# A transformer layer's feed-forward start: one token tile handled in two halves, transposes and operand splits moved in a written-out order

## The chip, the cores and the metric

One core of a Trainium2 chip runs the whole layer in one launch. The metric is the device time of one execution in microseconds (us), the median over several runs. The core's engines are TensorE (PE, with its weight loads PEld), VectorE (DVE), ScalarE (ACT), GpSimd (POOL) and SyncE (SP, which issues nearly all DMAs here).

## The reference

One layer of a backbone with 640 tokens (512 latent tokens in four tiles of 128, and one tile of 128 context tokens), width 1024, feed-forward width 2816. Two attention-like branches (a bidirectional recurrence and a neighbourhood attention) are merged; what matters here is what follows them:

```python
x = x + g1 * (merged @ p["w_out"])
h2 = _rmsnorm(x, p["norm2_g"]) * (1.0 + sc2) + sh2
x = x + g2 * ((jax.nn.silu(h2 @ p["ffn_w1"]) * (h2 @ p["ffn_w3"])) @ p["ffn_w2"])
```

`g1`, `sc2`, `sh2`, `g2` come from the conditioning vector, one set for the latent tokens and one for the context tokens.

## The kernel before

**Numbers.** Every large matrix product is made of three TensorE passes: an operand is split into a rounded high part, which ACT casts, and a low part, the difference, which DVE (or POOL) subtracts; the passes are high x high, high x low and low x high. `split` (L203 to L205) does this for activations, `wcast` (L185, L188) and `w_hl` (L1851, L1854) for weights. So each operand costs one ACT instruction, then one DVE instruction that waits for it.

**The stage.** The last part of the `w_out` product runs token tile by token tile (`acc`, L303), first tiles 0, 1, 2 together (72 matmuls), then tiles 3 and 4 (48). As a tile's product ends, `n_add` adds it to `x2`, `n_square`, `n_rstd` and `n_scale` normalise the tile, `n_out` transposes it on TensorE (L1739; four 128x128 blocks for each half `q` of the width, into a PSUM tile `xt` of a ring of three) and ACT (L1745) and DVE (L1747) scale and shift it out of PSUM into `hq[q, n]`, two blocks each; `n_split` splits that into `B2[q, n]`, high and low. `n` is the half of the tokens: 0 for tokens 0 to 319, 1 for 320 to 639. Token tile 2 lies across the border, so `cuts(2)` gives two pieces of 64 tokens.

**The first two hidden tiles** (`ft` 0 and 1) use `B2` directly: `conv_gen(ft, n)` makes two products, with `w1` and `w3`, of 24 matmuls each, in the order (0, 0), (1, 0), (0, 1), (1, 1). Their weights are `ffw[0]` to `ffw[3]`. `conv_out` applies silu (L1833, on ACT), multiplies (L1834, DVE) and splits the result into `u`. The tiles after them go through `pair`: seven products stand for eight, over sums and differences of weights (`w_sum`, L1865: `s1` to `s4`) and differences of the token halves. `t_sum` (L1769) makes these four differences in place in `hq`, `t_split` splits them into `BT[1]` to `BT[4]`. The weight operands of a pair are called a, b, c, d; `ha`, `la` are the high and low part of a, and so on.

**A detail of `pair`.** Its products run in the order a, b, a, b, c, b, c (the fourth b-type one uses weight d). The first a product ends in PSUM tile `A_`; ACT copies it out (`p1`, L1891), and the third product then adds on into the same `A_`. So the third product may start only when the copy `p1` has been made. In the table `wt`, `hc` (an ACT cast) stands ahead of `p` on ACT.

**The order.** TensorE, DVE, ACT and POOL run in the order in which the code emits. `beside` counts the matmuls of this stage and calls, at the numbers of the table `n2`, the steps that stand there, each a letter and an index:

| letter | step |
|---|---|
| A, S, R, X | `n_add`, `n_square`, `n_rstd`, `n_scale` of a token tile |
| T, U | `n_out` of a tile, width half 0 and 1 |
| H, J | `n_split` of a tile, width half 0 and 1 |
| W | load and split one of the weights `ffw` |
| D, E | `t_sum`, `t_split` |
| Y | `conv_out` (index 2 ft + n) |
| K | K0 issues the DMAs of the first pair's weights, K1 to K8 take the entries of `w0` in turn |

Matmuls 1 to 72 are tiles 0 to 2 of `w_out`, 73 to 120 tiles 3 and 4, 121 to 168 `conv_gen(0, 0)`, 169 to 216 `conv_gen(1, 0)`, 217 to 264 and 265 to 312 the two with n = 1. The four `hq` tiles and the two parts of `B2[0, 1]` lie in a ring "q" of six buffers, whose buffers the `u` tiles take over later in the order in which they were handed out.

Of the kernel before, what the change touches and what calls it, by code (L numbers as in the profile page):

```python
# [7 lines left out]
F32 = mybir.dt.float32  # L8
# [6 lines left out]
P = 128  # L15
NT = 640
NS = 512
H2 = 320
# [36 lines left out]
        "2 0 6 6 6 4 4 5 2 0 5 1 1 0 0"),  # L55
    qp=((0, 0, 7, 6, 7), (2, 5, 4, 4, 3, 2, 5, 3, 1)), ada=2, pa=1, pd=0,
    lw=(0, 0, 0, 0, 0, 2, 2, 2, 2, 2, 2, 2, 2, 2, 2, 2),
    n2=("48:A0S0 60:A1S1R0X0 72:A2S2R1X1 74:R2T0 76:U0X2H0J0 86:T1U1H1J1 89:W1 92:W0 100:T2U2H2J2 108:A3S3 "
     "120:A4S4R3X3R4X4W2W3 160:T3U3H3J3 180:T4U4H4J4 200:D1D3D2D4 210:E2E3E1 218:K0E4 "
     "230:Y0Y2K1K2K3K4K5K6K7K8 266:Y1"),  # L60
    te="dddddddd", pf=2, se="pddd", oe="d", w0="s3 s1 s2 s4 ha la hb lb",
    wt=(
        "<x -hc <h p -hd -lc <m",
        "u -ld <i <o",
# [43 lines left out]
def body(ctx: ExitStack, tc: tile.TileContext, xs, xp, cols, consts, w_ada, b_row, w_rw, w_qkv,  # L108
# [69 lines left out]
    def wcast(w, eng=None):  # L178
        st, n, pl, nhl = w
        hi = pl.tile([P, 1024], F32R, tag="whi", bufs=nhl, name=nm("whi"))  # L180
        lo = pl.tile([P, 1024], F32R, tag="wlo", bufs=nhl, name=nm("wlo"))
        if eng is pool:
            act.activation(lo[:, :n], st[:, :n], AF.Copy, scale=-1.0)
            pool.dma_start(lo[:, :n].bitcast(F32), st[:, :n], accum_op=ALU.add)
        act.copy(hi[:, :n], st[:, :n])  # L185
        if eng is not pool:
            def low(a, b):
                dve.tensor_tensor(out=lo[:, a:b], in0=st[:, a:b], in1=hi[:, a:b].bitcast(F32), op=ALU.subtract)  # L188

            if len(gtag) > 1:  # L190
                low(0, 512)
                later(lambda: low(512, n), (0, 0), -off[0] + 5)
            else:
                low(0, n)
        return hi, lo

    def wload(src, eng=None):
        return wcast(wdma(src), eng)
# [152 lines left out]
    s1 = ExitStack()  # L351
# [7 lines left out]
    p1 = sb  # L359
# [5 lines left out]
    pp = open_pool(s1a, "pp1a", bufs=2, space=PSUM)  # L365
# [6 lines left out]
    xt, q0 = [], []  # L372
# [61 lines left out]
    with s0:  # L434
        with tc.manual_schedule(engines=START):
            g = ada_part(0, 2, 0)
# [21 lines left out]
            g = ada_part(2, 2, 128)  # L458
# [7 lines left out]
            g = ada_part(4, 4, 256)  # L466
# [356 lines left out]
    with s1:  # L823
# [812 lines left out]
    pp = open_pool(ctx, "pp4", bufs=3, space=PSUM)  # L1636
# [27 lines left out]
    w0 = w_out_gen(pss, [c0] + [w_out[q] for q in range(1, 4)], range(5))  # L1664
# [20 lines left out]
    def add_gated(ps, i, n, c, a=0, b=512):  # L1685
# [10 lines left out]

    qp = open_pool(ctx, "qp")
    halves2 = [(q, n) for q in range(2) for n in range(2)]
    hq = {x: qp.tile([P, 4, H2], F32, tag="q", bufs=6, name=f"hq{x[0]}{x[1]}") for x in halves2}
    B2 = {x: [qp.tile([P, 4, H2], F32R, tag="q" if x == (0, 1) else f"b{x[0]}{x[1]}{i}", bufs=6 if x == (0, 1) else 1,  # L1700
                      name=f"b{x[0]}{x[1]}{i}") for i in range(2)] for x in halves2}
    sb = open_pool(ctx, "p4")
# [15 lines left out]
    nr = [{} for _ in range(5)]  # L1718
# [13 lines left out]
        dve.tensor_scalar(out=nr[i]["x"], in0=x2[i], scalar1=nr[i]["r"][:, 0:1], scalar2=None, op0=ALU.mult)  # L1732

    def n_out(i, q):
        g = 0 if i < 4 else 1
        ps = pp.tile([P, 512], F32, tag="tp", name=nm("xt"))
        for k in range(4):
            kt = 4 * q + k
            pe.transpose(ps[:, k * 128:(k + 1) * 128], nr[i]["x"][:, kt * 128:(kt + 1) * 128], ident)  # L1739
        for n, p0, p1, a in cuts(i):  # L1740
            for k in range(4):
                kt = 4 * q + k
                src, t = ps[:, k * 128 + p0:k * 128 + p1], hq[q, n][:, k, a:a + p1 - p0]
                if k < 2:
                    act.activation(t, src, AF.Identity, scale=m2[:, kt, g:g + 1], bias=s2[:, kt, g:g + 1])  # L1745
                else:
                    dve.tensor_scalar(out=t, in0=src, scalar1=m2[:, kt, g:g + 1],  # L1747
                                      scalar2=s2[:, kt, g:g + 1], op0=ALU.mult, op1=ALU.add)

    def cuts(i):  # L1750

        if i == 2:
            return (0, 0, 64, 256), (1, 64, 128, 0)
        return (((0, 0, 128, 128 * i),) if i < 2 else ((1, 0, 128, 128 * i - H2),))

    def n_split(i, q):
        for n, p0, p1, a in cuts(i):
            sl = slice(a, a + p1 - p0)
            split(*[B2[q, n][p_][:, :, sl] for p_ in range(2)], hq[q, n][:, :, sl],
                  pool if PRM["h2e"][2 * i + q] == "p" else dve)  # L1760
# [14 lines left out]
    def eng_x(c):  # L1775
        return pool if c == "p" else dve

    ffw = {}
    steps = dict(D=t_sum, E=t_split, Y=lambda i: conv_out(i), K=lambda i: first_prep(i), A=n_add, S=n_square, R=n_rstd, X=n_scale, T=lambda i: n_out(i, 0), U=lambda i: n_out(i, 1), H=lambda i: n_split(i, 0), J=lambda i: n_split(i, 1),
                 W=lambda i: ffw.update({i: wload(w13[i])}))  # L1780
    at, cnt = [(int(n), e) for n, e in (x.split(":") for x in PRM["n2"].split())], [0]

# [42 lines left out]
    def conv_out(i):  # L1825
        ft, n = i // 2, i % 2
        if i not in cps:
            return
        if n == 0:
            hidden(ft)  # L1830
        p1, p3 = cps.pop(i)
        a = sb.tile([P, NT], F32, tag="a", bufs=2, name=nm("a"))[:, :H2]
        act.activation(a, p1[:, :H2], AF.Silu)  # L1833
        dve.tensor_tensor(out=a, in0=a, in1=p3[:, :H2], op=ALU.mult)  # L1834
        sl = slice(H2 * n, H2 * n + H2)
        split(u[ft][:, 0, sl], u[ft][:, 1, sl], a)


    W = {}

    def w_stage(ft):
        W[ft] = dict(g=wdma(w13[2 * ft], 1), u=wdma(w13[2 * ft + 1], 0))

# [31 lines left out]
    def pair(ft, tag, old, now, nxt):  # L1875
# [215 lines left out]
```

## Time and profile before

| | |
|---|---|
| median of 3 runs | 1175.58 us (1175.09 to 1177.53) |
| profiled execution | 1175.43 us, of which the profile's span is 1173.7 us |
| mean granted TensorE clock | 0.991 |
| PE busy | 1125.1 us, 96% of the span |
| DVE busy | 778.6 us, 66% |
| ACT busy | 531.9 us, 45% |
| POOL busy | 193.2 us, 16% |
| the stage of the change | from about 715 us to 785 us of the span |
| the feed-forward part behind it | 785 us to the end |

Times in the profile's rows are microseconds from the span's start. A row of the timeline gives the start, the time from the first start to the last end of a merged group, the engine, the line, the operation, output and input tiles, the count, and in brackets the idle time of the engine ahead of it and what ended it. Matmuls follow each other faster than one lasts, so their pace is read from the starts. A row of the windows view gives, for a stretch, each engine's busy time, the granted clock (1.00 is full), the DMA engines' share and GB/s.

### The profile page before, as it was taken

The page shows a single profiled execution, that of the slowest core. Times are in us where ns is not written, and L with a number is a line of the kernel's source. Part 1 is how long each engine was busy: PE and PEld are TensorE (multiplying, and loading weights), DVE is VectorE, ACT ScalarE, POOL GpSimd, SP SyncE. Part 2 cuts the span into 40 slices and gives each one's busy share as a digit, 9 for nine tenths or more (in the row PEclk, how much of TensorE's full clock was granted, in tenths as well). Part 3 has the DMA queues.
Part 4 walks back from the last instruction along what each step waited for, and adds up shares of the span by engine and source line. Part 5 has one row for each costly group of instructions (what it writes and reads, how often), then busy time and mean ns, then how long its engine had stood idle before and what let it go on. Part 6 is the DMA issues. An engine that isn't in the chain of part 4 may idle for free.

```text
span 1173.7 us, 26876 instructions
## 1 busy us (share of the span) xinstructions
PE 1125.1 (96%) x11160; PEld 995.6 (85%) x11160; DVE 778.6 (66%) x1643; ACT 531.9 (45%) x1050; POOL 193.2 (16%) x260
## 2 busy tenths in 40 slices
PE   6999999999999999999899899999999999999998
PEld 4688877789888988888788777899899989998997
DVE  4565465559558747935576847887577756875775
ACT  4444666554564665556443324654224423441330
POOL 1162244320101202111100231100000000001000
PEclk9999999999999999999899999999999999999999
DMA  9752767554433523433843641312312222232122
GB/s 338 265 115 83 240 227 231 188 162 103 105 84 93 139 69 91 111 99 93 281 122 114 216 159 55 108 58 88 108 54 91 91 89 65 80 108 90 54 81 99
DMA packets 60194, 148.11 MB, mean 126 GB/s; under 512 B 7428, under 2 KB 22404, under 8 KB 60072
## 3 DMA queue, kind: packets, MB, share of 16 engines
q1 hardware_dynamic: 55464, 131.56, 34.3%
q0 software_dynamic: 3744, 13.63, 6.0%
q8 instruction: 88, 1.44, 0.5%
q10 hardware_dynamic: 864, 1.20, 0.4%
q14 instruction: 34, 0.28, 0.1%
HBM read 118.41 MB, written 14.32 MB: 113 GB/s over the span
## 4 chain that ended last, share of the span: by engine, by line
PE 60%; DVE 10%; ACT 3%; issue 2%; DMA 2%; SPq 0%; POOL 0%; DVEq 0%; ACTq 0%; POOLq 0%
PE f L1810 21%; PE acc L303 16%; PE fl L216 11%; PE w L1367 1%; PE w L1394 1%; DVE pr L1293 1%; PE w L1407 1%; PE mm L216 1%; PE w L1379 1%; PE w L1191 1%; DVE RL L1297 1%; DVE Rt L1327 1%; PE w L1424 1%; PE w L1385 1%; PE w L1239 1%
## 5 line engine op out<-in xcount | busy, mean ns | idle before, releaser
L1810 PE MATMUL f<-t,whi 128*128 128x320 f32 x640 | 142.4, 311 | 0.0
L1810 PE MATMUL f<-b,whi 128*128 128x320 f32 x608 | 135.6, 310 | 2.1 <-ACT b L204 1.8
L303 PE MATMUL acc<-whi,u 128*128 128x512 f32 (+1 forms) x448 | 136.0, 385 | 0.0
L216 PE MATMUL fl<-h,whi 128*128 128x320 f32 x672 | 121.2, 320 | 1.0 <-issue 1.0
L1810 PEld LDWEIGHTS f<-t,whi 128*128 128x128 f32 x640 | 108.1, 189 | 0.0
L185 ACT CAST whi<-wst 128x1024 fp32r<-128x1024 f32 (+1 forms) x77 | 79.1, 1033 | 62.3 <-PE acc L303 42.7
L216 PEld LDWEIGHTS fl<-h,whi 128*128 128x128 f32 x672 | 101.3, 188 | 5.8 <-issue 1.2
L1810 PEld LDWEIGHTS f<-b,whi 128*128 128x128 f32 x608 | 102.0, 188 | 3.3 <-ACT b L204 2.2
L1810 PE MATMUL f<-t,wlo 128*128 128x320 f32 x320 | 99.4, 310 | 0.0
L303 PEld LDWEIGHTS acc<-whi,u 128*128 128x128 f32 x448 | 83.5, 188 | 16.7
L1810 PE MATMUL f<-b,wlo 128*128 128x320 f32 x304 | 94.3, 310 | 2.2 <-DVE wlo L1854 2.2
L1851 ACT CAST whi<-ws 128x1024 fp32r<-128x1024 f32 x40 | 42.0, 1051 | 109.0 <-PE f L1810 44.4
L188 DVE TENSOR_TENSOR wlo<-wst,whi 128x1024 fp32r<-128x1024 f32 (+2 forms) x59 | 63.4, 1086 | 36.9 <-ACT whi L185 36.3
L303 PE MATMUL acc<-wlo,u 128*128 128x512 f32 (+1 forms) x224 | 86.3, 385 | 0.0
L1865 POOL TENSOR_TENSOR ws<-wst 128x512 f32<-128x512 f32 x20 | 28.0, 1402 | 340.8 <-DVE wlo L1854 226.7
L303 PE MATMUL acc<-whi,h 128*128 128x512 f32 x240 | 78.0, 399 | 0.9 <-DVE h L428 0.9
L216 PE MATMUL fl<-h,wlo 128*128 128x320 f32 x336 | 63.3, 321 | 0.0
L1688 DVE SCALAR_TENSOR_TENSOR tt<-acc,G 128x512 f32<-128x512 f32 (+1 forms) x51 | 34.5, 680 | 42.7 <-PE acc L303 42.7
L1851 ACT CAST whi<-wst 128x1024 fp32r<-128x1024 f32 (+1 forms) x48 | 41.3, 869 | 42.3 <-PE acc L303 25.1
L1810 PEld LDWEIGHTS f<-t,wlo 128*128 128x128 f32 x320 | 60.5, 189 | 0.0
L1810 PEld LDWEIGHTS f<-b,wlo 128*128 128x128 f32 x304 | 57.2, 188 | 2.5 <-DVE wlo L1854 2.5
L1854 DVE TENSOR_TENSOR wlo<-ws,whi 128x1024 fp32r<-128x1024 f32 x40 | 54.7, 1366 | 6.6 <-ACT whi L1851 6.6
(342 smaller groups left out, 2507.8 us busy)
## 6 DMA issues: line engine op xcount, KB each, us to landing
wst<-in_w_dram SPq DMA_DIRECT2D x66, 512.0 KB
wst<-in_w_rw_dram SPq DMA_DIRECT2D x31, 512.0 KB
wlo<-wst POOLq DMA_DIRECT2D x26, 512.0 KB, 4.8
wa<-in_w_ada_dram SPq DMA_DIRECT2D x24, 512.0 KB
f<-in_w_ada_dram SPq DMA_DIRECT2D x16, 512.0 KB
wst<-in_w_qkv_dram SPq DMA_DIRECT2D x12, 512.0 KB
o<-o_d SPq DMA_DIRECT2D x14, 320.0 KB
x<-in_xs_dram SPq DMA_DIRECT2D x8, 512.0 KB
```

The source lines that it names most:

```text
L185: act.copy(hi[:, :n], st[:, :n])
L188: dve.tensor_tensor(out=lo[:, a:b], in0=st[:, a:b], in1=hi[:, a:b].bitcast(F32), op=ALU.subtract)
L216: pe.matmul(ps[:, :t1 - t0], w[:, a:a + 128], x[:, k0 + kt, t0:t1], start=n == 0, stop=n == 3 * nk - 1)
L303: pe.matmul(pss[i][:, a:b], lhs(x, kt, ts_), w[:, cs_], start=ki == 0 and n == 0, stop=ki == last and n == 2)
L1191: pe.matmul(pr[h][hrows[h ^ i], o_], x[hrows[h], :], R_[hrows[h], l, :], start=True, stop=True)
L1239: pe.matmul(pt[h][hrows[h ^ i], o_], S.BK[l // 10][hrows[h], l % 10, i, :], idh(h), start=True, stop=True)
L1293: dve.tensor_tensor(out=prv, in0=V(RL[:, s + 1 + a, :], [[32, b - a], [0, s]], s), in1=V(RL[:, s, :], [[0, b - a], [1, s]]), op=ALU.mult)
L1688: dve.scalar_tensor_tensor(out=tt, in0=ps[:, a:b], scalar=c, in1=G[:, g, sl], op0=ALU.mult, op1=ALU.mult)
L1810: pe.matmul(ps[:, :H2], w_[:, c_], x_[:, kt, :], start=first and kt + n == 0, stop=last and kt == 3 and n == 2, skip_group_check=more)
L1851: act.copy(r[0][:, :width], src())
L1854: dve.tensor_tensor(out=r[1][:, :width], in0=src(), in1=r[0][:, :width].bitcast(F32), op=ALU.subtract)
L1865: eng_x(PRM["se"][i - 1]).tensor_tensor(out=o_, in0=x, in1=y, op=op)
```

## The change

It edits the table `n2`, the first entry of `w0`, the order in which the four `hq` buffers are handed out, and it lets `n_out` and `n_split` do the two pieces of token tile 2 one after the other: T2, U2, H2, J2 do the low piece (tokens 256 to 319), and new steps F2, G2 the high piece (tokens 320 to 383) from the same transposed PSUM tile.

```diff
-    n2=("48:A0S0 60:A1S1R0X0 72:A2S2R1X1 74:R2T0 76:U0X2H0J0 86:T1U1H1J1 89:W1 92:W0 100:T2U2H2J2 108:A3S3 "
-     "120:A4S4R3X3R4X4W2W3 160:T3U3H3J3 180:T4U4H4J4 200:D1D3D2D4 210:E2E3E1 218:K0E4 "
-     "230:Y0Y2K1K2K3K4K5K6K7K8 266:Y1"),
-    te="dddddddd", pf=2, se="pddd", oe="d", w0="s3 s1 s2 s4 ha la hb lb",
+    n2=("48:A0S0 60:A1S1R0X0 72:A2S2R1X1 74:R2T0 76:U0X2H0J0 86:T1U1H1J1 89:W1 92:W0 94:T2U2H2J2 104:F2G2 108:A3S3 "
+     "120:A4S4R3X3R4X4W2W3 174:T3U3H3J3 186:T4U4H4J4 204:D1D3D2D4K0E2Y0 218:E3Y2 232:K1K2K3K4K5K6K7K8 262:E1 266:Y1 280:E4"),
+    te="dddddddd", pf=2, se="pddd", oe="d", w0="ha s3 s1 s2 s4 la hb lb",
...
-    hq = {x: qp.tile([P, 4, H2], F32, tag="q", bufs=6, name=f"hq{x[0]}{x[1]}") for x in halves2}
+    hq = {x: qp.tile([P, 4, H2], F32, tag="q", bufs=6, name=f"hq{x[0]}{x[1]}") for x in ((1, 1), (0, 1), (0, 0), (1, 0))}
...
     def n_out(i, q):
-        g = 0 if i < 4 else 1
-        ps = pp.tile([P, 512], F32, tag="tp", name=nm("xt"))
+        ps = nr[i][q] = pp.tile([P, 512], F32, tag="tp", name=nm("xt"))
         for k in range(4):
             kt = 4 * q + k
             pe.transpose(ps[:, k * 128:(k + 1) * 128], nr[i]["x"][:, kt * 128:(kt + 1) * 128], ident)
-        for n, p0, p1, a in cuts(i):
+        n_mod(i, q, cuts(i)[:1])
+
+    def n_mod(i, q, cs_):
+        g, ps = 0 if i < 4 else 1, nr[i][q]
+        for n, p0, p1, a in cs_:
             for k in range(4):
...
-    def n_split(i, q):
-        for n, p0, p1, a in cuts(i):
+    def n_split(i, q, second=False):
+        if second:
+            n_mod(i, q, cuts(i)[1:])
+        for n, p0, p1, a in cuts(i)[1:] if second else cuts(i)[:1]:
...
+                 F=lambda i: n_split(i, 0, True), G=lambda i: n_split(i, 1, True),
```

No instruction is added or taken away on any engine. POOL's and SP's instructions stand in the same order as before, and so do those of all engines outside this stage. Three places follow, on DVE and on TensorE. In names, `hq01` is q = 0, n = 1; the third digit of `b001` is 0 for high and 1 for low; the numbers behind an underscore only tell buffers apart. Line numbers of the new kernel differ by one to five.

**DVE, the third token tile** (behind the low parts of `ffw[1]` and `ffw[0]`). Before:

```order
L1747 TENSOR_SCALAR hq00_9393<-xt_1274_9666,m2_9380,s2_9381 128x64 x2
L1747 TENSOR_SCALAR hq01_9394<-xt_1274_9666,m2_9380,s2_9381 128x64 x2
L1747 TENSOR_SCALAR hq10_9395<-xt_1275_9679,m2_9380,s2_9381 128x64 x2
L1747 TENSOR_SCALAR hq11_9396<-xt_1275_9679,m2_9380,s2_9381 128x64 x2
L205 TENSOR_TENSOR b001_9398<-hq00_9393,b000_9397 128x4x64
L205 TENSOR_TENSOR b011_9400<-hq01_9394,b010_9399 128x4x64
L205 TENSOR_TENSOR b101_9402<-hq10_9395,b100_9401 128x4x64
L205 TENSOR_TENSOR b111_9404<-hq11_9396,b110_9403 128x4x64
```

Now:

```order
L1749 TENSOR_SCALAR hq00_9395<-xt_1274_9660,m2_9380,s2_9381 128x64 x2
L1749 TENSOR_SCALAR hq10_9396<-xt_1275_9669,m2_9380,s2_9381 128x64 x2
L204 TENSOR_TENSOR b001_9398<-hq00_9395,b000_9397 128x4x64
L204 TENSOR_TENSOR b101_9402<-hq10_9396,b100_9401 128x4x64
L1749 TENSOR_SCALAR hq01_9394<-xt_1274_9660,m2_9380,s2_9381 128x64 x2
L204 TENSOR_TENSOR b011_9400<-hq01_9394,b010_9399 128x4x64
L1749 TENSOR_SCALAR hq11_9393<-xt_1275_9669,m2_9380,s2_9381 128x64 x2
L204 TENSOR_TENSOR b111_9404<-hq11_9393,b110_9403 128x4x64
```

The low piece of both width halves is now scaled and split ahead of the high piece; ACT's half of the work moved in the same way.

**TensorE, the fourth token tile's transposes** (`xt` out of the normalised tile `xn_1278`). Before they stand eight matmuls ahead of the end of `conv_gen(0, 0)`, whose second product is `f_1291`:

```order
L1810 MATMUL f_1291_9786<-b100_9401,whi_1269_9645 128x320
L1739 MATMUL xt_1292_9803<-K_67,xn_1278_9712 128x128 x4
L1739 MATMUL xt_1293_9812<-K_67,xn_1278_9712 128x128 x4
L1810 MATMUL f_1291_9786<-b101_9402,whi_1269_9645 128x320
L1810 MATMUL f_1291_9786<-b100_9401,wlo_1270_9646 128x320
```

Now they stand behind the first six matmuls of `conv_gen(1, 0)` (`f_1292`, weights `whi_1285`, `wlo_1286`, which are `ffw[2]`):

```order
L1815 MATMUL f_1292_9811<-b000_9397,whi_1285_9742 128x320
L1815 MATMUL f_1292_9811<-b001_9398,whi_1285_9742 128x320
L1815 MATMUL f_1292_9811<-b000_9397,wlo_1286_9743 128x320
L1737 MATMUL xt_1293_9818<-K_67,xn_1278_9712 128x128 x4
L1737 MATMUL xt_1294_9827<-K_67,xn_1278_9712 128x128 x4
```

So these eight transposes now come after TensorE's first use of `ffw[2]`, where they used to come ahead of it.

**DVE, around the first pair's low parts** (`wlo_1308` is `la` and `wlo_1310` `lb` before; `wlo_1327` is `lc`). Before, with all four differences split earlier:

```order
L1865 TENSOR_TENSOR ws_1306_9957<-wst_1299_9924,ws_1305_9956 128x512
L1854 TENSOR_TENSOR wlo_1308_9963<-wst_1299_9924,whi_1307_9962 128x1024
L1854 TENSOR_TENSOR wlo_1310_9967<-ws_1305_9956,whi_1309_9966 128x1024
L1834 TENSOR_TENSOR a_1313_10008<-a_1313_10008,f_1311_9980 128x320
L205 TENSOR_TENSOR u_1301_9944<-a_1313_10008,u_1301_9944 128x320
L1834 TENSOR_TENSOR a_1315_10060<-a_1315_10060,f_1314_10035 128x320
L205 TENSOR_TENSOR u_1303_9950<-a_1315_10060,u_1303_9950 128x320
L1854 TENSOR_TENSOR wlo_1327_10090<-ws_1306_9957,whi_1326_10089 128x1024
```

Now (`wlo_1306` is `la`, `t11` and `t41` are the splits E1 and E4):

```order
L1870 TENSOR_TENSOR ws_1308_9954<-wst_1298_9897,ws_1307_9953 128x512
L1859 TENSOR_TENSOR wlo_1306_9951<-wst_1298_9897,whi_1305_9950 128x1024
L1859 TENSOR_TENSOR wlo_1310_9961<-ws_1307_9953,whi_1309_9960 128x1024
L204 TENSOR_TENSOR t11_9996<-hq00_9395,t10_9995 128x1280
L1839 TENSOR_TENSOR a_1313_10004<-a_1313_10004,f_1311_9972 128x320
L204 TENSOR_TENSOR u_1300_9905<-a_1313_10004,u_1300_9905 128x320
L204 TENSOR_TENSOR t41_10024<-hq10_9396,t40_10023 128x1280
L1839 TENSOR_TENSOR a_1315_10060<-a_1315_10060,f_1314_10035 128x320
L204 TENSOR_TENSOR u_1303_9930<-a_1315_10060,u_1303_9930 128x320
L1859 TENSOR_TENSOR wlo_1327_10090<-ws_1308_9954,whi_1326_10089 128x1024
```

Two of the four splits moved from ahead of `la` to behind `lb`, between the outputs Y1 and Y3 of the first two hidden tiles; the other two, E2 and E3, now each stand ahead of Y0 and Y2. ACT's casts for E1 and E4 moved likewise, so that E4's cast and the casts behind Y1 and Y3 stand ahead of the copy `p1`.

## The prediction

> **What bounds the kernel now.** I read the page first, then the windows by stage, then who waited for whom on TensorE between 715 and 830 us, then the timelines of the three engines there. The page's busy times and two windows:
>
> ```profile
> PE 1125.1 (96%) x11160; PEld 995.6 (85%) x11160; DVE 778.6 (66%) x1643; ACT 531.9 (45%) x1050; POOL 193.2 (16%) x260
> ...
> 736.60:769.50 32.90, 30.88 (x211) 30.23 (x210) 28.58 (x45) 20.32 (x35) 4.08 (x4) 1.00 0.24 80
> ...
> 785.00:1173.00 388.00, 384.86 (x2275) 359.29 (x2273) 269.85 (x370) 126.58 (x174) 25.02 (x18) 1.00 0.26 85
> ```
>
> The columns are PE, PEld, DVE, ACT, POOL. TensorE bounds the whole; behind 785 us it idles 3 us in 388, so a microsecond lost before 785 us is a microsecond at the end. But from 737 to 769 us DVE is busy 28.6 of 32.9 us: here it is nearly a second bound. TensorE's waits in this stage:
>
> ```profile
> PE f L1810 <- DVE wlo L1854: 2.2, 1, 2.2
> PE f L1810 <- ACT b L204: 1.8, 1, 1.8
> PE f L1810 <- DVE b L205: 0.3, 1, 0.3
> ...
> PEld f L1810 <- ACT p L1891: 0.3, 1, 0.3
> ```
>
> These are two holes and one hint. In TensorE's timeline they stand so:
>
> ```profile
> 735.72 0.39 PE L303 MATMUL acc<-wlo,m 128*128 128x512 f32 x1
> ...
> 736.40 0.39 PE L303 MATMUL acc<-wlo,m 128*128 128x512 f32 x1
> 738.55 0.42 PE L1810 MATMUL f<-b,whi 128*128 128x320 f32 x1 [1.76 <-ACT b L204]
> 739.22 0.41 PE L1810 MATMUL f<-b,whi 128*128 128x320 f32 x1 [0.26 <-DVE b L205]
> 739.47 0.31 PE L1810 MATMUL f<-b,wlo 128*128 128x320 f32 x1
> ...
> 740.50 0.46 PE L1810 MATMUL f<-b,whi 128*128 128x320 f32 x2
> ...
> 745.05 1.03 PE L1739 MATMUL xt<-K,xn 128*128 128x128 f32 x8
> 745.84 0.40 PE L1810 MATMUL f<-b,whi 128*128 128x320 f32 x1
> ...
> 747.38 0.31 PE L1810 MATMUL f<-b,wlo 128*128 128x320 f32 x1
> ...
> 769.09 0.52 PE L1810 MATMUL f<-b,whi 128*128 128x320 f32 x2
> 771.81 0.41 PE L1810 MATMUL f<-b,wlo 128*128 128x320 f32 x1 [2.20 <-DVE wlo L1854]
> ...
> 773.75 0.73 PE L1810 MATMUL f<-t,whi 128*128 128x320 f32 x2
> ...
> 774.55 0.73 PE L1810 MATMUL f<-t,whi 128*128 128x320 f32 x2
> ...
> 776.52 0.31 PE L1810 MATMUL f<-t,wlo 128*128 128x320 f32 x1
> 776.87 0.57 PE L1810 MATMUL f<-b,whi 128*128 128x320 f32 x2
> ```
>
> Seven 320-wide matmuls take 740.50 - 739.47 = 1.03 us, 0.147 each; a 512-wide one takes (736.40 - 735.72) / 3 = 0.227. *First hole*: the feed-forward part could start at 736.63 and have its third matmul at 736.92; that came at 739.47, so 2.55 us are lost. *Second hole*: the third matmul of the first `pair`, due at 769.09 + 0.29 = 769.38, came at 771.81, when `la` was there: 2.43 us. *The hint*: from 773 us on three matmuls take 774.55 - 773.75 = 0.80 us, 0.267 each, nearly half speed, and yet the third product, which starts at 776.87, waited a little for the copy `p1`. At full speed it would have come at 771.81 + 0.25 + 21 x 0.147 = 775.15 and waited 1.7 us.
>
> **The third tile in halves.** DVE's and ACT's rows for the first hole and the weights behind it:
>
> ```profile
> 734.93 0.59 DVE L1747 TENSOR_SCALAR hq<-xt,m,s 128x64 f32<-128x64 f32 x2
> ...
> 738.76 1.42 DVE L205 TENSOR_TENSOR b<-hq,b 128x256 fp32r<-128x256 f32 x4
> ...
> 745.70 2.35 DVE L188 TENSOR_TENSOR wlo<-wst,whi 128x1024 fp32r<-128x1024 f32 x2
> 747.97 1.36 DVE L1747 TENSOR_SCALAR hq<-xt,m,s 128x128 f32<-128x128 f32 x4
> ```
> ```profile
> 738.10 1.31 ACT L204 CAST b<-hq 128x256 fp32r<-128x256 f32 x4
> ...
> 743.92 1.98 ACT L185 CAST whi<-wst 128x1024 fp32r<-128x1024 f32 x2
> 745.80 1.50 ACT L1745 ACTIVATE hq<-xt,s,m 128x128 f32<-128x128 f32 x4
> ```
>
> DVE still starts the tile at 734.93, behind the weights' low parts, so the transposes' six steps of lead (6 x 0.227 = 1.4 us) buy nothing. Two pairs (0.59 each, back to back about 1.1) end at 736.0; ACT's first cast (0.4) follows the first pair and is done by 736.0; DVE's two low parts (0.4 each) end near 736.4 and 736.9. TensorE needs the cast at 736.63, the first low part at 736.78, the second twelve matmuls on. The first hole closes: -2.55 us. The high piece then alternates, ACT and DVE waiting for each other at each step (0.59 + 0.4 + 0.4 for each half, with waits of 0.2 and 0.5 between them), and ends near 740.3, where the four low parts end now at 740.18: +0.1 for what DVE has queued behind it.
>
> **The next wait takes it.** DVE's low part of `ffw[2]` ends at 745.70 + 1.2 = 746.9 and keeps its place behind the tiles' sums and scalings; it moves by that 0.1, to 747.0. TensorE, 48 matmuls after 736.63, wants it at 743.7 + 0.3. So the third matmul of `conv_gen(1, 0)` starts at 747.05, against 747.38 now: of 2.55 us, 0.33 remain. And the fourth tile's eight transposes (745.84 - 745.05 = 0.79 us), done by then in the old order, still lie ahead. Net TensorE is 0.46 us later.
>
> Those transposes now start near 747.75, their first four end near 748.4, ACT's pair takes 0.8 (half of the row at 745.80), and DVE begins the tile at 749.25 instead of 747.97, having stood idle for 1.1 us: +1.28 for all DVE has queued behind it. The fifth tile follows within DVE's backlog and adds nothing. TensorE may wait at its last transposes for a buffer of the ring `xt`; ACT and DVE leave that buffer at about 750, TensorE comes at 750.8, so I take nothing (bounds 0 and 0.5).
>
> **The splits.**
>
> ```profile
> 753.94 6.14 DVE L1769 TENSOR_TENSOR hq<-hq,hq 128x1280 f32<-128x1280 f32 x4
> 760.00 5.69 DVE L205 TENSOR_TENSOR t<-hq,t 128x1280 fp32r<-128x1280 f32 x4
> ...
> 770.54 1.22 DVE L1854 TENSOR_TENSOR wlo<-wst,whi 128x1024 fp32r<-128x1024 f32 x1
> ```
> ```profile
> 758.58 4.75 ACT L204 CAST t<-hq 128x1280 fp32r<-128x1280 f32 x4 [5.28 <-DVE hq L1769]
> ...
> 775.08 0.46 ACT L204 CAST u<-a 128x320 fp32r<-128x320 f32 x1 [0.97 <-DVE a L1834]
> 775.45 1.05 ACT L1851 CAST whi<-ws 128x1024 fp32r<-128x1024 f32 x1
> ```
>
> The row at 775.45 is `hc`. `la` ends at 771.76. In the new order it gains two splits, 2 x 5.69 / 4 = 2.84, loses the 1.28, and loses about 0.7 because E3's cast (4.75 / 4 = 1.19) now stands on ACT behind Y0's cast while DVE waits: 771.76 - 2.84 + 1.28 + 0.7 = 770.9. TensorE is there at 769.38 + 0.46 = 769.8, so the second hole shrinks from 2.43 to about 1.1. TensorE so far stands 0.9 us better than before.
>
> **Then the copy `p1`.**
>
> ```profile
> 776.40 0.41 ACT L1891 COPY p<-f 128x320 f32<-128x320 f32 x1
> ```
>
> From the end of `la` to the end of `p1` it is 776.81 - 771.76 = 5.05 us now: `lb`, Y1 and Y3 on DVE, two casts, `hc`, the copy. In the new order DVE has E1 and E4 in this stretch, 2.84 more, and E4 waits about 0.4 for its cast, which stands behind Y1's on ACT. So `p1` ends at 770.9 + 5.05 + 3.2 = 779.2, and the third product starts at 779.25, not 776.87: **+2.4 us**, in a wait of about 4.9 us (it could start at 774.3). What was a saving ahead of `la` is paid back, with 1.28 + 0.7 + 0.4 on top, behind it. Behind 779.25 the splits and `lc` (at 780.2, wanted at 783) are in time and nothing else waits.
>
> Edits that cost nothing: `ha` first in `w0` (ACT's order shows it at the same place); K0 earlier (SP's order is unchanged, and its loads wait for buffers that the low parts of `ffw` free, which move by 0.1; a load that came late would cost as much); the order of the `hq` buffers (each `u` is cast behind the split that frees its buffer; without that order Y0 would wait for E1, a split of 1.4 us or more).
>
> **The clock.** The granted clock is the number behind the five engines' counts:
>
> ```profile
> 663.70:667.10 3.40, 1.32 (x9) 1.32 (x9) 3.40 (x7) 0.14 (x1) 0.00 (x0) 1.00 0.67 223
> 667.10:670.50 3.40, 3.25 (x9) 2.18 (x9) 3.40 (x6) 2.13 (x4) 2.77 (x3) 0.50 0.48 154
> ...
> 769.50:772.90 3.40, 1.20 (x8) 1.10 (x8) 3.37 (x5) 1.38 (x2) 0.00 (x0) 1.00 0.10 13
> 772.90:776.30 3.40, 3.40 (x15) 3.40 (x14) 2.12 (x4) 2.01 (x4) 1.28 (x1) 0.50 0.38 141
> ```
>
> Twice a stretch of 3.4 us in which TensorE idled over 2 us is followed by one of 3.4 us at clock 0.50; the first hole, 2 us, was not. Before, the slow stretch was hidden by the wait for `p1`. After a wait of 4.9 us the slow stretch falls behind it, on the path. A matmul there takes 0.267 instead of 0.147, so 45% of the slow time is lost: with 3.4 us 1.5, with 1.3 us (a stretch that began inside the wait) 0.6, with 4.7 us (one begun inside and a second) 2.1. I take 1.3, near the full stretch.
>
> [...]
>
> **Sum.** Profiled execution 1175.43 (0.15 under the median of the runs) + 2.4 + 1.3 = **1179.1 us**, bounds with this mechanism 1175.43 + 2.4 + 0.6 = 1178.4 and 1175.43 + 2.4 + 2.1 = 1179.9.
>
> **The rivals.**
> *No slow clock falls on the path*: the wait for `p1` alone, 1177.8, down to 1177.0 if E3's and E4's waits for ACT (0.7 + 0.4) are mostly hidden. For it: one hole of 2 us left the clock alone. Against it: two windows with more than 2 us did not, and this wait is twice as long. 0.16.
> *The clock halves at `ffw[2]` too*: TensorE waits there from 743.7 for the cast (ACT's row at 743.92, its first half done near 745.2) and again until 747.05, 3 us of 3.4; a slow stretch behind it delays the transposes of the fourth and fifth tile, to which DVE's backlog is tied, by up to 1 us, and so `p1`: 1180.1, with more slow clock behind `p1` 1181. 0.10.
> *Faster: `p1` is no limit.* If the third product does not wait for the copy, what decides is `la`: third matmul at 771.0, 22 more steps at full clock (the hole of 1.1 us is too short for the slow one), so the third product starts at 774.3 instead of 776.87: 1175.43 - 2.5 = 1172.9. It decides if the product need not wait until `p1` has read `A_`, or `p1` comes before 774.3. For it: the profile charges the copy with 0.3 us only. Against it: 776.87 is 0.06 us behind the copy's end, and the code adds into the tile that the copy reads. 0.08.
> *The halves don't get ahead* (a buffer or a wait holds the low piece until about 738.5 as now): TensorE comes to `ffw[2]` in time, but the transposes are later all the same and `p1` still moves by 1.5 to 2.4; 1177.5. 0.06.
>
> **How the numbers follow.** The forecast has 0.60. About 0.2%, 2.35 us, is what a measurement of this kernel can tell from no change. Slower by more: 0.60 + 0.10, half of the first rival and of the last, 0.81; within: the other halves, 0.11; faster: 0.08. The range takes in the forecast's bounds, the first rival to 1177.0 and most of the second to 1181.0; outside lie the faster rival and some tails.
>
> **What would show it.** Right: no wait at 736.6; a wait of about 3 us in all for `whi` L185 and `wlo` L188 near 744 to 747; DVE at the fourth tile about 1.3 us later; `la` a little earlier than 771.8 and a wait there of about 1 us; then a wait of nearly 5 us for the copy `p1`, and a stretch at clock 0.50 behind it. Wrong: the third product of the first pair starting before 777 us, or TensorE gaining at `ffw[2]`.

## The result, and the profile after

| | before | after |
|---|---|---|
| runs of this comparison | 8 | 8 |
| median | 1176.06 us (1175.09 to 1178.13) | 1181.76 us (1178.90 to 1185.00) |
| ratio, 95% interval | | 1.0045 [1.0032, 1.0057] |
| profiled execution (span) | 1175.43 (1173.7) | 1181.58 (1179.8) |
| mean granted clock of that execution | 0.991 | 0.991 |

The changed kernel is slower by 5.7 us; 1179.1 was forecast, with 1177.0 to 1181.0 as the range. The sign and the mechanism came as forecast, the size did not. A second comparison with the same kernel gave 1181.20 (10 runs) against 1176.90 (31 runs), ratio 1.0037 [1.0024, 1.0050]. The ratio and its interval are taken over all runs; the ratio is not the quotient of the two medians, which would be 1.0048 in the first comparison.

The page's busy times of the changed kernel, and TensorE's waits between 715 and 850 us:

```profile
PE 1124.9 (95%) x11160; PEld 996.4 (84%) x11160; DVE 779.9 (66%) x1643; ACT 532.3 (45%) x1050; POOL 193.8 (16%) x260
```
```profile
PE f L1815 <- ACT p L1896: 4.8, 1, 4.8
PE f L1815 <- DVE wlo L187: 1.4, 1, 1.4
PE f L1815 <- ACT whi L184: 1.3, 1, 1.3
PE f L1815 <- DVE wlo L1859: 1.1, 1, 1.1
```

The work is the same; the waits are others. The wait for the third tile (`b`) is gone, `ffw[2]` (L184, L187) took its place, the second hole (L1859) is half its size, and the wait for the copy `p1` is 4.8 us. TensorE's timeline, from the last matmul of `w_out` (738.29) on:

```profile
738.29 0.39 PE L302 MATMUL acc<-wlo,m 128*128 128x512 f32 x1
738.52 0.45 PE L1815 MATMUL f<-b,whi 128*128 128x320 f32 x2
...
746.98 0.55 PE L1815 MATMUL f<-b,whi 128*128 128x320 f32 x2 [1.26 <-ACT whi L184]
748.94 0.42 PE L1815 MATMUL f<-b,wlo 128*128 128x320 f32 x1 [1.41 <-DVE wlo L187]
...
749.64 1.03 PE L1737 MATMUL xt<-K,xn 128*128 128x128 f32 x8
...
773.18 0.42 PE L1815 MATMUL f<-b,wlo 128*128 128x320 f32 x1 [1.10 <-DVE wlo L1859]
...
781.45 0.75 PE L1815 MATMUL f<-b,whi 128*128 128x320 f32 x2 [4.76 <-ACT p L1896]
```

And the windows of 3.41 us around the last wait, in the order PE, PEld, DVE, ACT, POOL, granted clock, DMA share, GB/s:

```profile
774.83:778.24 3.41, 1.86 (x13) 1.59 (x11) 2.30 (x4) 1.96 (x3) 1.99 (x1) 1.00 0.30 117
778.24:781.66 3.42, 0.21 (x1) 0.21 (x2) 2.44 (x4) 1.99 (x4) 0.00 (x0) 1.00 0.00 0
781.66:785.07 3.41, 3.41 (x14) 3.41 (x14) 2.27 (x4) 0.36 (x2) 0.00 (x0) 0.50 0.21 47
785.07:788.48 3.41, 3.41 (x25) 3.41 (x24) 1.09 (x2) 1.76 (x3) 0.00 (x0) 1.00 0.29 114
```

The window in which TensorE was busy 0.21 us of 3.42 is followed by one at clock 0.50. This slow window lies behind the wait: 14 matmuls there, 25 in the window after.

**Where the time went.** The last matmul of `w_out` started 1.89 us later than in before's profile (738.29 against 736.40), by something ahead of the stage. So I count from that matmul. For every kernel of this study, in us behind it:

| kernel | last matmul of `w_out` at | third matmul of the pair (`la`) | third product | next pair | program's last matmul |
|---|---|---|---|---|---|
| before | 736.40 | 35.41 | 40.47 | 49.38 | 433.18 |
| after | 738.29 | 34.89 | 43.16 | 53.60 | 437.40 |
| after, again | 735.89 | 34.88 | 43.15 | 53.59 | 437.39 |
| halves_only | 739.99 | 35.50 | 40.55 | 49.45 | 433.25 |
| splits_only | 736.76 | 34.51 | 42.59 | 53.52 | 437.33 |
| splits_back | 738.33 | 38.43 | 44.05 | 52.85 | 436.64 |
| tiles_back | 735.87 | 33.74 | 42.01 | 53.29 | 437.09 |
| fill_wait | 736.25 | 34.91 | 43.19 | 52.10 | 435.90 |
| outs_later | 736.89 | 34.89 | 38.23 | 51.10 | 434.91 |
| outs_behind_z | 736.05 | 33.71 | 37.04 | 47.58 | 431.38 |
| outs_behind_w | 737.14 | 33.70 | 37.03 | 46.16 | 433.57 |
| before_put_off | 743.45 | 34.59 | 37.91 | 47.87 | 431.67 |

Inside the stage the change costs 437.40 - 433.18 = 4.22 us: 43.16 - 40.47 = 2.69 by the wait for `p1`, and 1.53 by the slow clock behind it. Behind the next pair's start nothing moves any more (383.80 us to the end in both).

### The profile page after: what moved, and what is told of

The parts are those of the page before. It is cut to its first block, busy times and chain, and to the rows that moved or that the text cites. A ratio compares the mean times of both kernels' runs of the same rounds, so it can differ in the third digit from the quotient of the medians.

```text
span 1179.8 us, 26874 instructions
## 1 busy us (share of the span) xinstructions
PE 1124.9 (95%) x11160; PEld 996.4 (84%) x11160; DVE 779.9 (66%) x1643; ACT 532.3 (45%) x1050; POOL 193.8 (16%) x260
## 4 chain that ended last, share of the span: by engine, by line
PE 60%; DVE 9%; ACT 4%; issue 3%; DMA 2%; SPq 0%; POOL 0%; DVEq 0%; ACTq 0%; POOLq 0%
PE f L1815 21%; PE acc L302 16%; PE fl L215 11%; PE w L1366 1%; PE w L1393 1%; PE mm L215 1%; PE w L1406 1%; PE w L1378 1%; DVE pr L1292 1%; PE w L1190 1%; DVE Rt L1326 1%; DMA wlo<-wst 1%; PE w L1423 1%; PE w L1384 1%; PE w L1238 1%
## 5 line engine op out<-in xcount | busy, mean ns | idle before, releaser
L184 ACT CAST whi<-wst 128x1024 fp32r<-128x1024 f32 (+1 forms) x77 | 79.2, 1033 | 61.1 <-PE acc L302 42.5
L187 DVE TENSOR_TENSOR wlo<-wst,whi 128x1024 fp32r<-128x1024 f32 (+2 forms) x59 | 64.7, 1109 | 36.3 <-ACT whi L184 35.8
L1859 DVE TENSOR_TENSOR wlo<-ws,whi 128x1024 fp32r<-128x1024 f32 x40 | 55.0, 1375 | 6.6 <-ACT whi L1856 6.6
```

The costliest lines, as they stand in the source:

```text
L1859: dve.tensor_tensor(out=r[1][:, :width], in0=src(), in1=r[0][:, :width].bitcast(F32), op=ALU.subtract)
```

## The experiments

**One part alone: the third tile in halves.** The kernel before, with

```diff
-100:T2U2H2J2
+94:T2U2H2J2 104:F2G2
```

> The kernel before with the third tile in two halves alone; all else in the old order. My theory: the first hole closes (2.0 to 2.5 us), but the third matmul of conv_gen(1, 0) still starts when the low part of ffw[2] is there, la and p1 move by 0.1: the third product starts 40.5 us behind the last matmul of w_out minus what that matmul gains, so at the same time as before, and the run takes 1176.7, the same as the kernel before; if the first hole of before halves the clock in some runs, up to 0.5 less. Rival (the halves pay by themselves): 1174.3.

Measured: 1178.06 us (11 runs) against 1176.90, ratio 1.0003 [0.9993, 1.0013]. TensorE's waits in the stage:

```profile
PE f L1816 <- DVE wlo L1860: 2.2, 1, 2.2
PE xt L1738 <- DVE rs L262: 1.8, 1, 1.8
```

The first hole is gone and a wait of 1.8 us has taken its place 8 us later: the transposes of the fourth tile wait for its normalisation (`rs`), which DVE finishes no earlier than before. Third product at 40.55 against 40.47, and the interval of the ratio contains 1: the halves alone change nothing that can be told, as expected. That TensorE would wait at the transposes, ahead of `ffw[2]`, I had not said.

**The other part alone: the order of sums, splits and outputs.**

```diff
-160:T3U3H3J3 180:T4U4H4J4 200:D1D3D2D4 210:E2E3E1 218:K0E4 230:Y0Y2K1...K8 266:Y1
+160:T3U3H3J3 180:T4U4H4J4 204:D1D3D2D4K0E2Y0 218:E3Y2 232:K1...K8 262:E1 266:Y1 280:E4
```

(with the changed kernel's `w0` and order of the `hq` buffers; `K1...K8` is short for the eight steps in turn)

> The kernel before with the new order of the sums, splits and outputs alone; the third tile whole and the transposes of the last two tiles where they were. My theory (what stands on DVE ahead of the copy p1 sets the third product): the first hole stays, la ends 2.1 us earlier (near 769.6) and the second hole is nearly gone, p1 ends 1.1 us later because E3 and E4 wait for their casts, the third product waits nearly 4 us for p1 and starts 1.1 us later than before, and a slow stretch of the clock behind it adds 0.6 to 1.5: 1177.5 to 1178.6 against 1176.1. Rival (only the late transposes cost): 1176.1, no slow clock on the path.

Measured: 1180.18 us (7 runs) against 1176.76, ratio 1.0031 [1.0019, 1.0043]. TensorE's waits, then the windows around the first hole and around the wait for `p1`:

```profile
PE f L1809 <- ACT p L1890: 4.7, 1, 4.7
PE f L1809 <- ACT b L203: 1.8, 1, 1.8
```
```profile
736.11:739.52 3.41, 1.45 (x6) 0.72 (x4) 2.06 (x8) 2.75 (x10) 0.00 (x0) 1.00 0.73 247
739.52:742.93 3.41, 3.30 (x12) 3.31 (x13) 3.34 (x8) 1.29 (x3) 0.00 (x0) 0.50 0.20 53
773.66:777.07 3.41, 1.00 (x7) 0.73 (x6) 2.30 (x4) 1.96 (x3) 1.06 (x1) 1.00 0.01 5
777.07:780.48 3.41, 1.13 (x4) 1.13 (x5) 2.43 (x5) 2.25 (x4) 0.00 (x0) 0.50 0.00 0
780.48:783.89 3.41, 3.41 (x15) 3.41 (x14) 1.36 (x3) 0.87 (x2) 0.00 (x0) 0.50 0.44 155
```

The rival, that only the late transposes cost, falls: to the end of the program this part alone costs 437.33 - 433.18 = 4.15 us in its profile, nearly all of the whole change's 4.22. The wait for `p1` is there, but the time lies above the forecast range (1177.5 to 1178.6): `la` comes 0.9 us earlier, not 2.1, and the third product is 2.12 us later than before, not 1.1. Part of this belongs to this execution: its first hole was followed by a slow stretch (739.52), behind which the transposes came later; DVE began the four sums 0.7 us later than in before (755.01 - 736.76 against 753.94 - 736.40). Behind the wait stood 783.89 - 779.35 = 4.5 us of slow clock, and not 3.4: here it cost 2.0.

**The splits back ahead of `la`, the rest of the change kept.**

```diff
-218:E3Y2 232:K1...K8 262:E1 266:Y1 280:E4
+218:E3Y2E1E4 232:K1...K8 266:Y1
```

> The changed kernel with E1 and E4 split ahead of la again, the rest (halves, late transposes, Y0 and Y2 between E2 and E3) kept. My theory (the copy p1 is as late as DVE's work ahead of it, in whatever order): la comes 2.6 to 2.9 us later, p1 comes 0.4 to 1 us earlier because E4 no longer waits for its cast; the wait is split into one of nearly 4 us at la and one under 2 us at p1, so most of the slow stretch falls ahead of p1, where it is hidden: 0.5 less for p1 and about 1 less for the clock, 1180 against 1181.5. Rival (putting the splits behind la is what costs the 2.7): 1178 to 1179, p1 2.4 us earlier.

Measured: 1180.24 us (11 runs) against 1176.90, ratio 1.0028 [1.0017, 1.0039]; the changed kernel in the same comparison 1181.20. TensorE and ACT:

```profile
772.76 0.56 PE L1815 MATMUL f<-b,whi 128*128 128x320 f32 x2 [0.94 <-ACT whi L1856]
776.76 0.63 PE L1815 MATMUL f<-b,wlo 128*128 128x320 f32 x1 [3.45 <-DVE wlo L1859]
...
782.38 0.46 PE L1815 MATMUL f<-b,whi 128*128 128x320 f32 x2
```
```profile
781.35 0.42 ACT L1896 COPY p<-f 128x320 f32<-128x320 f32 x1
```

This is the test of "what was a saving ahead of `la` is paid back behind it". `la` comes 3.5 us later, and the copy at 781.35 - 738.33 = 43.02, where the changed kernel has it at 780.98 - 738.29 = 42.69 (its row stands below). The copy is as late as DVE's work ahead of it, in whichever order; the rival (2.4 us earlier) falls. That the copy would come 0.4 to 1 us earlier was wrong too: E1 now waits 0.7 us for its cast. The slow stretch came ahead of the third product (three matmuls in 778.00 - 777.20 = 0.80 us) and hid the copy, as in the kernel before; from the third product on three take 782.82 - 782.38 = 0.44 us, the pace of the full clock. This version gains 0.75 us in the stage against the changed kernel (52.85 against 53.60).

**The transposes back.**

```diff
-174:T3U3H3J3 186:T4U4H4J4
+160:T3U3H3J3 180:T4U4H4J4
```

> The changed kernel with the transposes of the fourth and fifth tile back at matmuls 160 and 180. My theory: DVE begins the fourth tile without its 1.1 us of idleness, so all behind it, p1 too, comes 1.3 us earlier: 1180.4 against 1181.8 of the changed kernel; the wait for p1 and the slow clock behind it stay. Rival (the splits alone cost, DVE catches up by then): 1181.8.

Measured: 1181.43 us (6 runs) against 1176.76, ratio 1.0042 [1.0027, 1.0057]: too wide to tell 1.3 us. The profile tells it: `la` and the third product come 1.15 us earlier (33.74 and 42.01). But the wait now fell so that slow stretches of 776.37 to 783.19 lay around it:

```profile
772.96:776.37 3.41, 0.14 (x1) 0.00 (x0) 2.47 (x3) 1.79 (x4) 0.29 (x1) 1.00 0.00 0
776.37:779.78 3.41, 1.90 (x7) 1.90 (x8) 2.74 (x5) 1.97 (x4) 0.00 (x0) 0.50 0.02 5
779.78:783.19 3.41, 3.41 (x15) 3.41 (x14) 0.58 (x1) 1.37 (x2) 0.00 (x0) 0.50 0.44 156
```

From the third product (777.88) to 783.19 the clock was 0.50, 5.3 us at a price of 2.4 instead of 1.5: of 1.15 us, 0.31 were left at the end of this execution.

**Work in the wait.** Behind the first pair's second product:

```diff
+            if ft == FA and j == 1:
+                for _ in range(2):
+                    for _ in mm4(C_, w["b"], 0, BT[2]):
+                        pass
```

> The changed kernel with 24 more matmuls of 320 columns behind the second product of the first pair, 3.5 us at full clock, into the tile of the third result, which the fifth product overwrites: TensorE works in the wait for p1, and nothing comes later. My theory (waiting halves the clock): no slow stretch behind the wait, the third product starts where it did and the products behind it go at 0.147 instead of 0.267: 1.5 us less, 1180.3 against 1181.8. Rival (the slow clock has another cause, or the 5.7 us are waits alone): no change, or 1 us slower if the fill runs past the copy.

Measured: 1180.15 us (9 runs) against 1176.76, ratio 1.0029 [1.0019, 1.0040].

```profile
777.86 0.31 PE L1815 MATMUL f<-t,wlo 128*128 128x320 f32 x1
779.44 0.57 PE L1815 MATMUL f<-b,whi 128*128 128x320 f32 x2 [1.27 <-ACT p L1896]
...
781.31 0.46 PE L1815 MATMUL f<-t,whi 128*128 128x320 f32 x2
```

The third product starts where it did (43.19), but its twelve matmuls take 781.31 - 779.44 = 1.87 us instead of 784.67 - 781.45 = 3.22, from 779.99 to 791.43 every three matmuls take 0.44 us, the pace of the full clock, and the next pair starts at 52.10 instead of 53.60. 24 needless matmuls gain 1.50 us in the profile: the slow clock behind the wait is caused by TensorE's idleness in it, and that was its price. (The runs agree, but with overlapping intervals: 1.0029 here, 1.0045 and 1.0037 for the changed kernel.)

**The changed kernel again.**

> The changed kernel once more. My theory (what the first profile had beyond 4.2 us, 1.9 us of them ahead of the stage, is where the slow stretches happened to fall): ahead of the stage the profile stands within 1 us of before's 736.40, inside the stage it loses 4 to 5.5 us, and the runs' median is 1180.5 to 1181.5, 4 to 5 above before. Rival (the change costs something ahead of the stage as well): the stage begins 1.5 to 2 us late again and the median is 1182.

Measured: 1181.20 us (10 runs) against 1176.90. Its timeline:

```profile
735.89 0.39 PE L302 MATMUL acc<-wlo,m 128*128 128x512 f32 x1
...
779.04 0.65 PE L1815 MATMUL f<-b,whi 128*128 128x320 f32 x2 [4.76 <-ACT p L1896]
```

The stage begins 0.5 us earlier than in before's profile, where the first profile had begun it 1.9 later; inside the stage both agree within 0.01 us. So the 1.9 us were that execution's, not the change's.

**The work that nobody waits for, put off.** E4, Y1 and Y3 leave the table and are called inside the first pair, behind the addition `u`:

```diff
-262:E1 266:Y1 280:E4
+262:E1
...
-        "u -ld <i <o",
+        "u -e4 -ld -y1 -y3 <i <o",
```

> The changed kernel with E4, Y1 and Y3 emitted inside the first pair, behind the copy p1 and the addition u: nothing that the first four products can do without stands ahead of p1. My theory: p1 comes right behind the first product, the third product starts 22 steps behind la, about 5 us earlier than in the changed kernel, and the slow stretch goes: 6.5 us less, 1175.2, below the kernel before (1176.1) by 1 to 2.5 us. Rival (p1 was no limit, the third product waits for something else): no change, 1181.8. Second rival: E4, needed at the sixth product, or the next pair's weights, now late, take back 1 to 2 us: 1177.

Measured: 1177.67 us (12 runs) against 1176.76, ratio 1.0013 [1.0003, 1.0023].

```profile
PE f L1816 <- DVE u L1892: 2.1, 1, 2.1
```

`p1` was the limit: the third product comes at 38.23, 4.9 us earlier, as forecast. The time did not come as forecast (1175.2), because 2.1 us came back at the sixth product, which waits for the addition `z` (in the row `u`, its output's name), now behind Y1 and Y3 on DVE; a slow stretch followed that wait (from 784.03 to 786.43 every three matmuls take 0.80 us). What I had named as what might take it back (E4, the next pair's weights) was not what did.

**The same, behind `z`, and the transposes back.** Against the changed kernel, `n2` has the transposes at 160 and 180 again and neither Y1 nor E4, and the table `wt` puts E4, Y1 and Y3 into the first pair. Y3's tile behind silu (`a`) also takes another buffer, that of the pair's `c2`.

```diff
-174:T3U3H3J3 186:T4U4H4J4 ... 262:E1 266:Y1 280:E4
+160:T3U3H3J3 180:T4U4H4J4 ... 262:E1
...
-        "u -ld <i <o",
+        "u -e4 -ld <i <o",
...
-        "z >s2 >ha",
+        "z -y1 -y3 >s2 >ha",
```

> A version meant to beat both: the changed kernel with the transposes of the last two tiles back at 160 and 180, E4 inside the first pair behind the addition u, and Y1 and Y3 behind the addition z. My theory: no wait for p1 and none for z; the third product starts 37 us behind the last matmul of w_out (40.5 in before, 43.2 in the changed kernel), the next pair 46 to 46.5 us (49.4 and 53.6), perhaps with a wait under 0.5 us for v or the next pair's la; no slow stretch of the clock on the path: 1173.5 against 1176.7 of before. Rival (DVE's work that was put off makes the next pair wait instead): 1175.5 or more.

Measured: 1174.76 us (9 runs) against 1176.90, ratio 0.9978 [0.9966, 0.9990]: faster than both kernels.

```profile
744.09 1.09 PE L1737 MATMUL xt<-K,xn 128*128 128x128 f32 x8 [1.79 <-DVE rs L261]
769.76 0.41 PE L1816 MATMUL f<-b,wlo 128*128 128x320 f32 x1 [0.80 <-DVE wlo L1860]
781.77 0.56 PE L1816 MATMUL f<-b,whi 128*128 128x320 f32 x2 [1.28 <-DVE c L1892]
```

The third product stands at 37.04 as forecast; the addition `v` (output `c`), behind Y1 and Y3, makes the seventh product wait 1.28 us, where I had allowed 0.5, so the stage gives 1.80 us against the kernel before, not 3.

**Is anything of the change needed for that?** The kernel before, with E4 behind `u` and Y1, Y3 behind `z`, by the same edits of `wt` and with the same buffer for Y3's tile as in the version above, and nothing else:

```diff
-210:E2E3E1 218:K0E4 230:Y0Y2K1...K8 266:Y1
+210:E2E3E1 218:K0 230:Y0Y2K1...K8
```

> The kernel before with one thing alone: E4 inside the first pair behind u, Y1 and Y3 behind z; no halves, no later transposes, E1 to E3 ahead of la as before. My theory (what counts is only what stands on DVE ahead of la and p1): la ends 1.4 us earlier, 34.0 us behind the last matmul of w_out instead of 35.4, TensorE waits there 1 us and not 2.2, no slow stretch follows, p1 is no limit, the third product starts at 37.2 (40.5 in before) and the next pair at 47.3 to 47.6 with the wait of 1.3 us for v (49.4 in before): 1174.8 against 1176.9. Rival (the gain of the last version needs the halves too): 1176.5 or more.

Measured: 1173.75 us (13 runs) against 1176.04, ratio 0.9979 [0.9970, 0.9988]. The same gain; the rival falls. Its profiled execution, at 1180.97 the slowest of the 13, began the stage 7 us late and yet gained 433.18 - 431.67 = 1.51 us from there to the end:

```profile
743.45 0.39 PE L303 MATMUL acc<-wlo,m 128*128 128x512 f32 x1
745.64 0.41 PE L1811 MATMUL f<-b,whi 128*128 128x320 f32 x1 [1.80 <-ACT b L204]
...
789.46 0.56 PE L1811 MATMUL f<-b,whi 128*128 128x320 f32 x2 [0.90 <-DVE c L1887]
```

There is no wait at `p1`. There is none at `la` either, where I had expected 1 us: here too the first hole was followed by a slow stretch (745.98 to 749.39, clock 0.50), so TensorE itself came later, and the third product stands at 37.91 and not 37.2.

**One step more: Y3 behind `w`.** On top of the version behind `z`, and with Y3's tile in the buffer of `p1` instead of that of `c2`:

```diff
-        "z -y1 -y3 >s2 >ha",
+        "z -y1 >s2 >ha",
...
-        "w >hb >lb",
+        "w -y3 >hb >lb",
```

> The last version with Y3 behind the addition w instead of z, so that v is not behind it. My theory: the wait of 1.3 us for v at the seventh product goes, the next pair starts 46.3 us behind the last matmul of w_out instead of 47.6: 1173.4 against 1174.7. Rival: Y3 now stands ahead of the next pair's low part of b, or its late product tile holds up the next pair: TensorE waits there instead and the time stays at 1174.7.

Measured: 1176.86 us (11 runs) against 1176.04, ratio 1.0010 [1.0002, 1.0019]. The rival is right about the wait, and the time is worse than it said.

```profile
786.07 0.57 PE L1816 MATMUL f<-t,whi 128*128 128x320 f32 x2 [0.85 <-ACT whi L1858]
787.33 0.41 PE L1816 MATMUL f<-t,wlo 128*128 128x320 f32 x1 [0.69 <-DVE wlo L1861]
...
788.12 0.73 PE L1816 MATMUL f<-t,whi 128*128 128x320 f32 x2
```
```profile
783.62 0.44 ACT L1840 ACTIVATE a<-f 128x320 f32<-128x320 f32 x1 [2.80 <-DVE c L1893]
```

The next pair starts 1.4 us earlier (46.16), and then waits for its own `hb` and `lb`, which are behind Y3; a slow stretch follows there (three matmuls in 788.92 - 788.12 = 0.80 us), and the program's last matmul comes 2.2 us later than with Y3 behind `z`. The buffer has a part in it: Y3's silu (783.62) began only when the addition `w` had read `p1`, after 2.80 us of idleness on ACT, and DVE then waited 0.56 us for it. How much of the loss is the buffer's and how much the place's, no run separates.

## Why the prediction was wrong in size and right in kind

- *The first hole closes*: right. 738.52 follows 738.29 without a wait.
- *`ffw[2]` takes it*: right, nearly to the hundredth. The third matmul of `conv_gen(1, 0)` starts 748.94 - 738.29 = 10.65 us behind `w_out`, before 10.98: the 0.33 that was said to remain.
- *DVE begins the fourth tile 1.28 later*: right, 1.26, with the 1.1 us of idleness. These are DVE's and ACT's rows:

```profile
751.12 1.43 DVE L1749 TENSOR_SCALAR hq<-xt,m,s 128x128 f32<-128x128 f32 x4 [1.10 <-ACT hq L1747]
...
771.91 1.22 DVE L1859 TENSOR_TENSOR wlo<-wst,whi 128x1024 fp32r<-128x1024 f32 x1
```
```profile
780.98 0.42 ACT L1896 COPY p<-f 128x320 f32<-128x320 f32 x1
```

- *`la` earlier by 0.86*: 0.52 (773.13 - 738.29 = 34.84 against 771.76 - 736.40 = 35.36). From its end to that of the copy it is 781.40 - 773.13 = 8.27, and 5.05 + 3.2 = 8.25 was forecast. So the wait's term, +2.4, measured +2.69; the 0.3 is `la`'s.
- *The slow clock behind the wait, 1.3*: 1.53 in both profiles of the changed kernel, a full stretch; 2.0 and 2.4 in two experiments. Taking the wait's idleness away took it away.
- *The sum*: this is the step that failed, in its first term, the 1175.43 of the kernel before, and in the range, which left no room for what differs from execution to execution. 1175.43 + 4.22 is 1179.65, inside the bounds that I gave the mechanism (1178.4 to 1179.9); the terms 2.4 and 1.3 were 0.5 short together. The profiled execution took 1181.58: the other 1.9 us stood ahead of the stage. 1175.43 was one execution, and the median of three runs beside it (1175.58) was no better a base: the kernel before has medians of 1176.06, 1176.76, 1176.90 and 1176.04 in four comparisons of 8, 23, 31 and 23 runs, 0.6 to 1.5 above 1175.43. With the second comparison's base 1176.90 + 4.22 = 1181.12, and 1181.20 was measured; with the first one's it is 1180.28, and 1181.76 was measured. And I put the scatter ahead of the stage at nothing: in the twelve profiles of this study the last matmul of `w_out` started between 735.87 and 743.45. The changed kernel's first profile stood 1.9 us late at that point and its repetition 0.5 early. What makes this scatter is not shown. Slow windows of the clock lie ahead of the stage, but their number does not tell these two profiles apart: before's (736.40) and the changed kernel's first (738.29) have five each, at 233.60, 342.83, 568.11, 571.52 and 667.09 and at 23.90, 245.77, 344.75, 570.03 and 706.57. As ratios, the forecast is 1.0031; the first comparison's interval begins just above it, the second one's contains it.
- *"One hole of 2 us left the clock alone"*, which I held for the first rival, was that execution's luck: in two other profiles the same hole was followed by a slow stretch (`splits_only` from 739.52, `before_put_off` from 745.98, both at clock 0.50). The rivals "`ffw[2]` halves the clock" and "`p1` is no limit" did not show: at `ffw[2]` and behind it the changed kernel's clock stayed at 1.00 (744.11 to 754.35), and the second is refuted by the wait of 4.8 us and by the versions that take work from ahead of the copy.
- What I read past: that the third product would wait for DVE's work I saw, but not that the same rows hold the remedy. Of the 8.27 us between `la` and the copy, one split and two outputs (Y1, E4, Y3 in DVE's order) take 780.65 - 775.58 = 5.07 with their waits for casts, and are wanted later:

```profile
775.58 0.48 DVE L1839 TENSOR_TENSOR a<-a,f 128x320 f32<-128x320 f32 x1
...
777.75 1.49 DVE L204 TENSOR_TENSOR t<-hq,t 128x1280 fp32r<-128x1280 f32 x1 [0.58 <-ACT t L203]
779.16 0.48 DVE L1839 TENSOR_TENSOR a<-a,f 128x320 f32<-128x320 f32 x1
780.16 0.49 DVE L204 TENSOR_TENSOR u<-a,u 128x320 fp32r<-128x320 f32 x1 [0.52 <-ACT u L203]
```

What stays open: the medians lie 4.3 and 5.7 us apart where the stage accounts for 4.2. As a ratio 4.22 us is 1.0036, inside both intervals, so the rest can be chance: ahead of the stage, or in slow stretches inside it that are longer in some executions. Only two executions of the changed kernel were profiled. In the eight runs of the first comparison the slowest had the lowest mean granted clock (1185.00 us, 0.984) and the fastest the highest (1178.90 us, 0.996); in the kernel before's 23 runs beside `splits_only` time and clock hardly go together (correlation -0.15). Another remedy was not tried: the copy `p1` reads only the first product, whose last matmul ended at 774.93, and stood on ACT behind casts that wait for DVE. No run moved the copy alone ahead of them.

## What to carry to other kernels

Where two engines are both near their bound, as here, moving one engine's work from ahead of one consumer to ahead of the next moved the wait and did not shorten it. What helped was to put the work that no consumer needed yet behind them, and the next thing to read is then the next consumer in that engine's queue (here `z`, then `v`, then the next pair's weights). An idle time of TensorE can cost more than its length: here 1.5 to 2.4 us of slow clock on top where one followed it. When a forecast is a few tenths of a per cent, take the base from many runs and give the range the scatter of that base, for one execution's time contains its own luck.

## What the runs showed of the hardware

The slow stretches lie on a grid whose phase differs from execution to execution. In the kernel before's profile they start at 233.60 and 32, 98, 127, 158 and 275 steps behind it, a step being (772.90 - 233.60) / 158 = 3.413 us; in the changed kernel's first at 23.90 and 65, 94, 160, 200, 222 and 339 steps behind it, with (781.66 - 23.90) / 222 = 3.413. Counted back to the span's start, the first grid's first line is at 1.49 us, the second's at 0.01. In `splits_only` 739.52 and 777.07 lie 11 steps apart.

The same idle time could be followed by the halved clock or not: the first hole left TensorE 1.65 us busy in its window on that grid in before's profile (735.36 to 738.77) and the next window was at 1.00; in `splits_only` it left 1.45 and the next was at 0.50. Of the windows measured on the grid in this stage, these were followed by clock 0.50: 0.14 us busy (`tiles_back`, from 772.96), 0.21 (changed kernel, 778.24), 0.33 (`after_again`, 775.96), 1.00, 1.13 and 1.45 (`splits_only`, 773.66, 777.07 and 736.11), 1.21 (before, 769.49), 1.61 (`before_put_off`, 742.57) and 1.90 (`tiles_back`, 776.37); those of 1.13 and 1.90 were at 0.50 themselves. These were followed by 1.00: 1.65 (before, 735.36), 1.74 (`after_again`, 772.54), and in the changed kernel's first profile 1.86 (774.83), 2.01 (747.52), 2.15 (744.11) and 2.31 (771.42, with the wait of 1.10 us in it). TensorE's busy time is not all of it: ahead of the stage that same profile has a window with 2.31 us busy (703.15 to 706.57) that was followed by 0.50 too.

In the version behind `z`, a low part (`lc`) took 2.32 us on DVE where one of its size takes 1.22, while POOL's `ws` took 2.43 where it takes 1.30:

```profile
770.76 1.48 DVE L204 TENSOR_TENSOR t<-hq,t 128x1280 fp32r<-128x1280 f32 x1
772.16 2.32 DVE L1860 TENSOR_TENSOR wlo<-ws,whi 128x1024 fp32r<-128x1024 f32 x1
```
```profile
770.98 2.43 POOL L1871 TENSOR_TENSOR ws<-wst 128x512 f32<-128x512 f32 x1 [18.77 <-issue]
785.06 1.30 POOL L1871 TENSOR_TENSOR ws<-wst 128x512 f32<-128x512 f32 x1 [11.66 <-DVE wlo L1860]
```

POOL ends at 773.41, 1.2 us behind the end of DVE's split at 772.24, and DVE's low part ends 1.07 us behind POOL. The version `outs_behind_w` has the same pair (2.32 from 773.24 on DVE, 2.43 from 772.06 on POOL). Why both take longer there is not shown. No run here took POOL's operation away, so its price on the path is not known.
